# The gate products and sums of squares of one group of heads: from GpSimd to VectorE

## The chip, the cores and the metric

The kernel runs on one core of one Trainium2 chip. Times are device microseconds (us) of one execution of the whole program. The engines are TensorE (PE in the profile, its weight loads PEld), VectorE (DVE), ScalarE (ACT), GpSimd (POOL) and SyncE (SP, which here only starts transfers). Each engine runs its own list of instructions in order; semaphores make one wait for another.

## The reference, cut to what matters

A trunk of two post-norm residual layers over 16 learned tokens and 256 frames, width 2048, in float32. The first layer mixes gated linear attention and stick-breaking attention, the second is a Mamba-2 (SSD) mixer with 8 groups of 8 heads. The change lies in the second. For each group, with `y` the scan's output of 512 channels and `z` the gate path:

```python
    y = _ssd(xs, bs, cs, dt, a_log, d_skip)
    y = _rms_norm_groups(y * jax.nn.silu(z), norm_w, SSM_GROUPS)
    return jnp.einsum('bte,ed->btd', y, w_out)
...
def _rms_norm_groups(y, w, n_groups):
    yg = y.reshape(*shp[:-1], n_groups, shp[-1] // n_groups)
    yg = yg * lax.rsqrt(jnp.mean(yg * yg, -1, keepdims=True) + RMS_EPS)
    return yg.reshape(shp) * w
```

So each group needs the product of `y` with the gate, and the mean of the squares of that product over the 512 channels.

## The kernel before, in words

Everything is computed channels on partitions, tokens along the free axis. The weights are streamed from memory in units of 128 by 2048 (`load_unit`, L144, on SyncE's queue, three `raw` buffers). A unit is used as an input projection (128 output channels against 16 slices of 128 inputs) or as part of an output projection. To keep float32 accuracy on TensorE's faster path every operand is split in a high and a low part: ScalarE copies the rounded value (`whi`, L159), VectorE subtracts (`wlo`, L160; some halves on GpSimd). A unit is split in two halves into five buffers of each kind; then `in_unit` runs 16 times three matmuls (L178 to L180: high by high, low by high, high by low) into one `pj` buffer of PSUM, 48 matmuls in all. The names in the rows are `pj_9759` and so on, one number for each unit's result.

In the second layer the plan lists the units of group 0 (B, C, four x, four z), those of group 1, and then for each further group its units and the four output units of the group two before. Between the matmuls of units, work of other tasks (generators stepped by `tick`) is put in: `decay1` makes the decay matrix `M` of a group (L1125 and L1126, then an exponential, then L1153, a product with `cb`, which GpSimd's masks of L249 have made causal), `x_path` transposes x (L1193, L1197 on TensorE) and scales it to `xd` (L1206, L1212), and `mix_ssd` multiplies both (L1255, L1261 on TensorE into two `po` buffers) and makes the group's output.

In `mix_ssd`, for each of four slices of 128 channels: VectorE adds the skip term (L1265, tile `yu`), GpSimd multiplies with the gate (L1266), ScalarE makes the high part `yh` (L1268) and the square (L1271, L1274), VectorE the low part `yl` (L1269), GpSimd adds the squares up in `ysq` (L1275). TensorE then sums `ysq` over the channels (L1281, against ones, in a `po` buffer), and VectorE begins the reciprocal root with L1286. `po` has two buffers, taken in turn: two for L1255's results of a group, one for L1281, then two for L1193 of the next group, and so on.

The order of instructions on each engine is chosen when the program is built: a scheduler (the tile framework with `schedule_with_timeline_sim=True`) plays the program through with estimated times and lists instructions as they become ready; `pin` keeps some of TensorE's in program order and `high_priority` moves some ahead. So a moved instruction can move others, on all engines.

Of the kernel before, what the change touches and what calls it, by code (L numbers as in the profile page):

```python
# [9 lines left out]
ALU = mybir.AluOpType  # L10
# [72 lines left out]
def _wait(*tasks):  # L83
    for t in tasks:
        while not t.done:
            yield


class _Body:
# [1146 lines left out]
    def mix_ssd(self, g):  # L1236
        nc, lp = self.nc, self.lp
        act, vec, mm = nc.scalar.activation, nc.vector, nc.tensor.matmul
        M, xt, z = self.cur["M", g], self.cur["x", g], self.cur["z", g]
        xd = self.cur["xd", g]  # L1240
        yield from _wait(self.tasks["decay", g], *[self.tasks[a, g, j] for a in "xz" for j in (1, 3)])
        yh, yl = self.mix[g] = self.y_tiles() if g else self.y0
        sq = lp.tile([P, S], F32, tag="ysq", name=self.nm("ysq"))
        for j in range(4):
            if j == 0:
                pin = self.tc.keep_in_program_order
                for _ in range(3):
                    yield
                os = [self.po() for _ in range(2)]
                gk = dict(skip_group_check=True)  # L1250
                ov = [o.rearrange("p (j t) -> p j t", j=2) for o in os]
                for s, t0, c0, c1 in ((0, 0, 0, 256), (1, 112, 256, 400)):
                    for h in range(HPG):
                        p, jj, i = h // 4, h // 2 % 2, h % 2
                        pin(mm(  # L1255
                            ov[p][i * 64 : (i + 1) * 64, jj, t0:S], xd[:, s, h * 64 : (h + 1) * 64], M[:, h, c0:c1],
                            start=(s, jj) == (0, 0), stop=False, **gk,
                        ))
                for n in range(4):
                    p, i = n // 2, n % 2  # L1260
                    pin(mm(ov[p][i * 64 : (i + 1) * 64, :, 240:S], self.xd2[:, n, :], self.mt2[:, n], start=False, stop=True, **gk))  # L1261
                yield
            o = os[j // 2][:, (j % 2) * S : (j % 2 + 1) * S]
            u = lp.tile([P, S], F32, tag="yu", name=self.nm("yu"), bufs=2)
            vec.scalar_tensor_tensor(u, xt[:, j, NM:T], self.col(C_DS, 4 * g + j), o, op0=ALU.mult, op1=ALU.add)  # L1265
            nc.gpsimd.tensor_tensor(u, u, z[:, j, :], op=ALU.mult)  # L1266
            w = self.col(C_ON, 4 * g + j)
            act(yh[:, j, :], u, AF.Identity, scale=w)  # L1268
            vec.scalar_tensor_tensor(yl[:, j, :], u, w, yh[:, j, :].bitcast(F32), op0=ALU.mult, op1=ALU.subtract)  # L1269
            if j == 0:  # L1270
                act(sq, u, AF.Square)  # L1271
            else:
                s2 = lp.tile([P, S], F32, tag="ys2", name=self.nm("ys2"), bufs=2)
                act(s2, u, AF.Square)  # L1274
                nc.gpsimd.tensor_tensor(sq, sq, s2, op=ALU.add)  # L1275
            yield
        for _ in range(4):
            yield
        ps = self.po()
        for t in range(2):  # L1280
            mm(ps[:, 16 * t : 16 * t + 16], sq[:, t * P : (t + 1) * P], self.ones[:, :16], start=True, stop=True)  # L1281
        m = lp.tile([P, 2], F32, tag="rm", name=self.nm("rm"))
        tmp = lp.tile([P, 2], F32, tag="rt", name=self.nm("rt"))
        r = lp.tile([P, 2], F32, tag="rr", name=self.nm("rr"), bufs=3)
        self.rstd1[g] = r
        vec.tensor_scalar(m, ps[:, 0:32:16], 1.0 / 512, RMS_EPS, op0=ALU.mult, op1=ALU.add)  # L1286
        act(r, m, AF.Ln)
        act(r, r, AF.Exp, scale=-0.5)
        self.newton(r, m, tmp)
        yield  # L1290
# [188 lines left out]
```

## Time and profile before

| what | value |
|---|---|
| time, median of 3 runs (lowest, highest) | 1383.4 us (1382.73, 1383.68) |
| the profiled execution's own time | 1386.69 us |
| span of the profiled execution, first to last instruction | 1385.0 us |
| mean granted clock of TensorE | 0.998 |
| busy: TensorE, weight loads, VectorE, ScalarE, GpSimd | 99%, 96%, 74%, 55%, 19% |

The profile shows one execution. "Busy" counts instructions running; the time that an instruction spends held by another engine counts as its own. In a timeline a row can hold several like instructions (x2, x4); its duration is then from the first start to the last end. What stands in square brackets is the engine's idle time before it and what ended it. Where an engine runs back to back, the distance between two starts is the true cost of the first. Matmuls overlap: their durations are longer than the distance between their starts. [...] The second layer begins at about 680 us, group 0's output is made between about 790 and 806 us.

### The profile page before, as it was taken

How to read it: one execution, taken by the hardware profiler on the slowest of the kernel's cores; microseconds unless marked ns; L12 is line 12 of the kernel's file. 1: busy time of each engine (PE TensorE's matmuls, PEld its weight loads, DVE VectorE, ACT ScalarE, POOL GpSimd, SP SyncE). 2: the span in 40 equal slices, each digit the busy share in tenths (PEclk: the TensorE clock that was granted, in tenths of full speed). 3: DMA queues.
4: the chain of work that ended last, by engine and by line, in shares of the span. 5: the costliest groups of instructions: out<-in, count | busy, mean ns of one | idle time of the engine just before them, and what ended most of it. 6: DMA issues, size and time to landing. Idle time of an engine off the chain costs nothing.

```text
span 1385.0 us, 26232 instructions
## 1 busy us (share of the span) xinstructions
PE 1374.1 (99%) x10643; PEld 1323.9 (96%) x10643; DVE 1030.8 (74%) x1762; ACT 768.3 (55%) x1141; POOL 263.1 (19%) x253
## 2 busy tenths in 40 slices
PE   9999999999999999999999999999999999999998
PEld 8999999999999999999999999899898999989986
DVE  7858576576565674568899999787877778867687
ACT  6646455355345544556587667656565655656551
POOL 0000100100101100004401143331322323133221
PEclk9999999999999999999999999999999999999999
DMA  9656446546455545554355655465555555455561
GB/s 329 209 172 201 163 163 206 169 155 227 153 173 171 169 161 191 172 165 161 123 183 197 231 181 205 169 244 182 209 177 195 190 191 222 169 198 183 181 214 61
DMA packets 61945, 256.73 MB, mean 185 GB/s; under 512 B 26176, under 2 KB 29056, under 8 KB 33408
## 3 DMA queue, kind: packets, MB, share of 16 engines
q1 hardware_dynamic: 61104, 254.27, 53.3%
q8 instruction: 83, 1.36, 0.4%
q10 hardware_dynamic: 720, 0.79, 0.2%
q14 instruction: 38, 0.31, 0.1%
HBM read 249.29 MB, written 5.74 MB: 184 GB/s over the span
## 4 chain that ended last, share of the span: by engine, by line
PE 94%; DVE 4%; DMA 1%; issue 1%; POOL 0%; ACT 0%; SPq 0%; ACTq 0%; DVEq 0%; POOLq 0%
PE pj L179 25%; PE pj L178 25%; PE pj L180 25%; PE pj L494 4%; PE pj L496 4%; PE pj L495 4%; PE po L1255 1%; PE po L631 1%; DVE wlo L160 1%; PE po L1193 0%; DMA raw<-in_wts 0%; DVE M L1125 0%; PE z L1143 0%; DVE xt L1070 0%; DVE acc L503 0%
## 5 line engine op out<-in xcount | busy, mean ns | idle before, releaser
L178 PE MATMUL pj<-xhi,whi 128*128 128x272 f32 (+4 forms) x2560 | 732.1, 286 | 1.7 <-ACT xhi L330 0.8
L179 PE MATMUL pj<-xlo,whi 128*128 128x272 f32 (+4 forms) x2560 | 730.8, 286 | 0.0
L180 PE MATMUL pj<-xhi,wlo 128*128 128x272 f32 (+4 forms) x2560 | 730.1, 286 | 0.0
L159 ACT ACTIVATE whi<-raw 128x1024 fp32r<-128x1024 f32 (+2 forms) x434 | 449.2, 1039 | 398.3 <-PE pj L179 326.3
L160 DVE TENSOR_TENSOR wlo<-raw,whi 128x1024 fp32r<-128x1024 f32 (+2 forms) x405 | 503.4, 1247 | 209.6 <-ACT whi L159 199.6
L178 PEld LDWEIGHTS pj<-xhi,whi 128*128 128x128 f32 x2560 | 482.6, 189 | 4.3 <-ACT whi L159 1.1
L179 PEld LDWEIGHTS pj<-xlo,whi 128*128 128x128 f32 x2560 | 482.6, 189 | 1.2 <-issue 0.6
L180 PEld LDWEIGHTS pj<-xhi,wlo 128*128 128x128 f32 x2560 | 482.6, 189 | 0.8 <-issue 0.8
L178 PE MATMUL pj<-mixh,whi 128*128 128x272 f32 x384 | 111.0, 290 | 0.0
L180 PE MATMUL pj<-mixh,wlo 128*128 128x272 f32 x384 | 110.7, 289 | 0.0
L179 PE MATMUL pj<-mixl,whi 128*128 128x272 f32 x384 | 110.7, 288 | 0.0
L160 POOL TENSOR_TENSOR wlo<-raw,whi 128x1024 fp32r<-128x1024 f32 x29 | 73.1, 2520 | 193.7 <-ACT whi L159 193.7
L494 PE MATMUL pj<-whi,yh 128*128 128x512 f32 (+1 forms) x240 | 93.3, 389 | 0.0
L495 PE MATMUL pj<-wlo,yh 128*128 128x512 f32 (+1 forms) x240 | 92.6, 386 | 0.0
L496 PE MATMUL pj<-whi,yl 128*128 128x512 f32 (+1 forms) x240 | 92.2, 386 | 0.0
L261 POOL TENSOR_TENSOR gr<-gr,gsc 128x1088 f32<-128x1088 f32 x6 | 15.4, 2574 | 303.6 <-ACT gsc L260 303.6
L179 PEld LDWEIGHTS pj<-mixl,whi 128*128 128x128 f32 x384 | 72.4, 188 | 0.2
L180 PEld LDWEIGHTS pj<-mixh,wlo 128*128 128x128 f32 x384 | 72.3, 188 | 0.0
L178 PEld LDWEIGHTS pj<-mixh,whi 128*128 128x128 f32 x384 | 72.2, 188 | 0.2
L503 DVE SCALAR_TENSOR_TENSOR acc<-pj,rr,acc 128x512 f32<-128x512 f32 (+1 forms) x65 | 46.5, 733 | 13.9 <-PE pj L496 13.9
L496 PEld LDWEIGHTS pj<-whi,yl 128*128 128x128 f32 x240 | 45.1, 188 | 9.2
L494 PEld LDWEIGHTS pj<-whi,yh 128*128 128x128 f32 x240 | 45.1, 188 | 8.9
(347 smaller groups left out, 1462.4 us busy)
## 6 DMA issues: line engine op xcount, KB each, us to landing
raw<-in_wts SPq DMA_DIRECT2D x212, 1024.0 KB, 4.8
ebc<-edr SPq DMA_DIRECT2D x8, 1664.0 KB, 6.4
raw<-in_wts SPq DMA_DIRECT2D x9, 256.0 KB, 6.3
vdr<-vt SPq DMA_DIRECT2D x8, 256.0 KB, 5.2
vt<-vdr SPq DMA_DIRECT2D x32, 64.0 KB, 2.4
hacc<-in_xT SPq DMA_DIRECT2D x7, 272.0 KB, 5.3
early<-in_wts SPq DMA_DIRECT2D x2, 512.0 KB, 7.7
vdr<-vt SPq DMA_DIRECT2D x8, 128.0 KB, 3.4
```

The lines of the kernel that those rows point to most:

```text
L159: self.nc.scalar.activation(hi, src, AF.Copy)
L160: eng.tensor_tensor(lo, src, hi.bitcast(F32), op=ALU.subtract)
L178: mm(ps, whi, xhi, start=first, stop=False)
L179: mm(ps, whi, xlo, start=False, stop=False)
L180: mm(ps, wlo, xhi, start=False, stop=last)
L261: mul(c, c, e, op=ALU.mult)
L494: mm(ps, yh[:, kk, tt], hi[:, k, :], start=kk == 0, stop=False)
L495: mm(ps, yh[:, kk, tt], lo[:, k, :], start=False, stop=False)
L496: mm(ps, yl[:, kk, tt], hi[:, k, :], start=False, stop=kk == 3)
L503: self.nc.vector.scalar_tensor_tensor(a, ps, r[:, t : t + 1], a, op0=ALU.mult, op1=ALU.add)
L631: mm = lambda r, a, b, start=False, stop=False: self.nc.tensor.matmul(o[:, r], a, b, start=start, stop=stop, skip_group_check=True)
L1255: pin(mm(ov[p][i * 64 : (i + 1) * 64, jj, t0:S], xd[:, s, h * 64 : (h + 1) * 64], M[:, h, c0:c1], start=(s, jj) == (0, 0), stop=False, **gk,))
```

## The change

For group 0 of the second layer, the four gate products and the three sums of squares are issued on VectorE, with the same operands. Groups 1 to 7 keep GpSimd. The first layer is not touched: only `mix_ssd`, which belongs to the second, changes.

```diff
@@ -1263,7 +1263,8 @@
             o = os[j // 2][:, (j % 2) * S : (j % 2 + 1) * S]
             u = lp.tile([P, S], F32, tag="yu", name=self.nm("yu"), bufs=2)
             vec.scalar_tensor_tensor(u, xt[:, j, NM:T], self.col(C_DS, 4 * g + j), o, op0=ALU.mult, op1=ALU.add)
-            nc.gpsimd.tensor_tensor(u, u, z[:, j, :], op=ALU.mult)
+            side = vec if g < 1 else nc.gpsimd
+            side.tensor_tensor(u, u, z[:, j, :], op=ALU.mult)
             w = self.col(C_ON, 4 * g + j)
             act(yh[:, j, :], u, AF.Identity, scale=w)
             vec.scalar_tensor_tensor(yl[:, j, :], u, w, yh[:, j, :].bitcast(F32), op0=ALU.mult, op1=ALU.subtract)
@@ -1272,7 +1273,7 @@
             else:
                 s2 = lp.tile([P, S], F32, tag="ys2", name=self.nm("ys2"), bufs=2)
                 act(s2, u, AF.Square)
-                nc.gpsimd.tensor_tensor(sq, sq, s2, op=ALU.add)
+                side.tensor_tensor(sq, sq, s2, op=ALU.add)
             yield
```

One line is added, so line numbers behind it are one higher in the changed kernel (L1266 is L1267 there, L1281 is L1282).

The scheduler's order moves with it. On TensorE, at the place where group 0's squares are summed over the channels (`ysq_9284` into `po_9540`) and group 1's x is transposed, before the change inside the unit pj_9759 (the third z unit of group 1):

```order
 L178 MATMUL pj_9759<-xhi,whi_9726 128x256
 L179 MATMUL pj_9759<-xlo,whi_9726 128x256
-L1281 MATMUL po_9540<-ones,ysq_9284 128x16 x2
-L1193 MATMUL po_9777<-ident,xt_9353 128x128 x4
 L180 MATMUL pj_9759<-xhi,wlo_9727 128x256
```

and now inside pj_9988 (the C unit of group 2):

```order
 L178 MATMUL pj_9988<-xhi,whi_9914 128x260
 L179 MATMUL pj_9988<-xlo,whi_9914 128x260
+L1282 MATMUL po_9540<-ones,ysq_9284 128x16 x2
+L1193 MATMUL po_9777<-ident,xt_9353 128x128 x4
 L180 MATMUL pj_9988<-xhi,wlo_9915 128x260
```

The sum over the channels stands the rest of pj_9759 (7 matmuls), the 48 of pj_9853, the 48 of pj_9913 and two of pj_9988 later, and group 1's first transposes with it; the second ones and L1255 of group 1 follow some 18 matmuls behind it.

On VectorE, from the second half of pj_9759's split on (`wlo_9727`); `yu_9378`, `yu_9396`, `yu_9420` and `yu_9440` are group 0's four slices, `M_9564` is group 1's decay matrix. Before:

```order
L1070 SCALAR_TENSOR_TENSOR xt_9353<-pj_9523,cpk,xt_9353 128x271
L160 TENSOR_TENSOR wlo_9727<-raw_9612,whi_9726 128x1024
L1269 SCALAR_TENSOR_TENSOR yl_8237<-yu_9378,cpk,yh_8236 128x256
L1070 SCALAR_TENSOR_TENSOR xt_9353<-pj_9523,cpk,xt_9353 128x270
L1269 SCALAR_TENSOR_TENSOR yl_8237<-yu_9396,cpk,yh_8236 128x256
L1265 SCALAR_TENSOR_TENSOR yu_9420<-xt_8545,cpk,po_9332 128x256
L1070 SCALAR_TENSOR_TENSOR xt_9353<-pj_9523,cpk,xt_9353 128x269
L1265 SCALAR_TENSOR_TENSOR yu_9440<-xt_8545,cpk,po_9332 128x256
L1081 TENSOR_TENSOR xt_9353<-xt_9353,xcl_9471 128x544
L1077 TENSOR_SCALAR xcl_9636<-xt_9353 128x544
L160 TENSOR_TENSOR wlo_9761<-raw_9687,whi_9760 128x1024
L160 TENSOR_TENSOR wlo_9813<-raw_9687,whi_9812 128x1024
```

Now, from the sum of the first two slices' squares on:

```order
L1276 TENSOR_TENSOR ysq_9284<-ysq_9284,ys_1126_9401 128x256
L1153 TENSOR_TENSOR M_9564<-M_9564,cb_9721 128x800
L1077 TENSOR_SCALAR xcl_9636<-xt_9353 128x544
L1153 TENSOR_TENSOR M_9564<-M_9564,cb_9721 128x800 x3
L1159 TENSOR_TENSOR mt_8239<-mt,cb_9721 16x2x16
L160 TENSOR_TENSOR wlo_9813<-raw_9687,whi_9812 128x1024
L1265 SCALAR_TENSOR_TENSOR yu_9420<-xt_8545,cpk,po_9332 128x256
L1159 TENSOR_TENSOR mt_8239<-mt,cb_9721 16x2x16 x3
L1265 SCALAR_TENSOR_TENSOR yu_9440<-xt_8545,cpk,po_9332 128x256
L160 TENSOR_TENSOR wlo_9855<-raw_9757,whi_9854 128x1024
```

The product with `cb` (L1153), which stood behind both splits of the next unit, now stands ahead of the second one (`wlo_9813`) and ahead of the third and fourth slices, whose last sum of squares comes five splits L160 later still (behind `wlo_9855`, `wlo_9883`, `wlo_9915`, `wlo_9952` and `wlo_9990`). On GpSimd the seven instructions of group 0 are gone, and the three masks L249 of `cb` follow directly on the product for group 1's B and C (L1081).

## Rows read from the trace of the kernel before

**Rows 1.** The page: the busy times of part 1 (share of the span, number of instructions), and the first line of part 4, the chain that ended last by engine.

```profile
PE 1374.1 (99%) x10643; PEld 1323.9 (96%) x10643; DVE 1030.8 (74%) x1762; ACT 768.3 (55%) x1141; POOL 263.1 (19%) x253
...
PE 94%; DVE 4%; DMA 1%; issue 1%; POOL 0%; ACT 0%; SPq 0%; ACTq 0%; DVEq 0%; POOLq 0%
```

**Rows 2.** The waits of TensorE over the whole span, longest first: who waited for whom, us in total, times, longest.

```profile
PE po L1281 <- POOL ysq L1275: 2.1, 1, 2.1
PE po L1413 <- ACT diag L1348: 1.2, 1, 1.2
```

**Rows 3.** TensorE's timeline around the wait: start, duration, engine, line, operation, and the idle time before it in brackets. The first two rows are the first and last of twelve matmuls in a row, from 807.59 up to the row of 810.45 there are thirteen.

```profile
802.83 0.28 PE L180 MATMUL pj<-xhi,wlo 128*128 128x256 f32 x1
...
804.08 0.28 PE L179 MATMUL pj<-xlo,whi 128*128 128x256 f32 x1
806.41 0.62 PE L1281 MATMUL po<-ones,ysq 128*128 128x16 f32 x4 [2.06 <-POOL ysq L1275]
806.88 1.06 PE L1193 MATMUL po<-ident,xt 128*128 128x128 f32 x4
807.59 0.56 PE L180 MATMUL pj<-xhi,wlo 128*128 128x256 f32 x1
...
810.45 0.28 PE L178 MATMUL pj<-xhi,whi 128*128 128x256 f32 x1
```

**Rows 4.** Windows of 2 us: busy time and count of PE, PEld, DVE, ACT and POOL, then the granted clock of TensorE, the DMA engines' busy share and GB/s.

```profile
806.00:808.00 2.00, 1.59 (x10) 1.59 (x11) 2.00 (x2) 2.00 (x5) 0.36 (x1) 0.73 0.25 98
808.00:810.00 2.00, 2.00 (x11) 2.00 (x11) 1.95 (x8) 1.38 (x3) 0.00 (x0) 0.50 0.00 0
810.00:812.00 2.00, 2.00 (x18) 2.00 (x17) 2.00 (x5) 0.67 (x3) 0.00 (x0) 0.91 0.00 0
```

**Rows 5.** GpSimd's timeline between 740 and 806 us.

```profile
748.93 3.01 POOL L249 TENSOR_SCALAR_AFFINE_SELECT cb<-cb 128x112 f32<-128x112 f32 x3 [74.34 <-ACT cb L1146]
...
790.92 1.62 POOL L1266 TENSOR_TENSOR yu<-yu,gz 128x256 f32<-128x256 f32 x2 [20.80 <-DVE yu L1265]
794.92 1.87 POOL L1275 TENSOR_TENSOR ysq<-ysq,ys 128x256 f32<-128x256 f32 x1 [2.38 <-ACT ys L1274]
798.40 5.21 POOL L1266 TENSOR_TENSOR yu<-yu,gz 128x256 f32<-128x256 f32 x2 [1.61 <-DVE yu L1265]
803.57 0.67 POOL L249 TENSOR_SCALAR_AFFINE_SELECT cb<-cb 128x112 f32<-128x112 f32 x3
804.20 2.15 POOL L1275 TENSOR_TENSOR ysq<-ysq,ys 128x256 f32<-128x256 f32 x2
```

**Rows 6.** VectorE's timeline in the same stretch: a pair of L1153, the rows beside GpSimd's first pair of products, and the rows around the second up to the next pause.

```profile
775.42 1.87 DVE L1153 TENSOR_TENSOR M<-M,cb 128x800 f32<-128x800 f32 x2
...
791.10 0.78 DVE L1126 TENSOR_SCALAR M<-ebc,est 128x144 f32<-128x144 f32 x1
791.80 0.88 DVE L1125 TENSOR_SCALAR M<-ebc,est 128x256 f32<-128x256 f32 x1
792.61 0.28 DVE L1126 TENSOR_SCALAR M<-ebc,est 128x144 f32<-128x144 f32 x1
792.81 0.34 DVE L1125 TENSOR_SCALAR M<-ebc,est 128x256 f32<-128x256 f32 x1
...
794.55 0.48 DVE L1070 SCALAR_TENSOR_TENSOR xt<-pj,cpk,xt 128x271 f32<-128x271 f32 x1
...
798.18 0.48 DVE L1070 SCALAR_TENSOR_TENSOR xt<-pj,cpk,xt 128x269 f32<-128x269 f32 x1
798.59 0.46 DVE L1265 SCALAR_TENSOR_TENSOR yu<-xt,cpk,po 128x256 f32<-128x256 f32 x1
798.98 0.70 DVE L1081 TENSOR_TENSOR xt<-xt,xcl 128x544 f32<-128x544 f32 x1
799.62 0.42 DVE L1077 TENSOR_SCALAR xcl<-xt 128x544 f32<-128x544 f32 x1
799.97 2.34 DVE L160 TENSOR_TENSOR wlo<-raw,whi 128x1024 fp32r<-128x1024 f32 x2
804.12 4.88 DVE L1153 TENSOR_TENSOR M<-M,cb 128x800 f32<-128x800 f32 x4 [1.81 <-POOL cb L249]
```

**Rows 7.** ScalarE's timeline: the copy of `cb`, and the split of the unit after pj_9913 (the one that waited for the end of pj_9853).

```profile
797.20 0.49 ACT L1146 ACTIVATE cb<-z 128x416 f32<-128x416 f32 x1
...
815.31 1.06 ACT L159 ACTIVATE whi<-raw 128x1024 fp32r<-128x1024 f32 x1 [0.38 <-PE pj L179]
```

**Rows 8.** TensorE's timeline: the first matmul of pj_9913, transposes in its middle at full clock and the matmul behind them, and the first matmul of pj_9988.

```profile
815.23 0.29 PE L178 MATMUL pj<-xhi,whi 128*128 128x272 f32 x1
...
817.09 0.60 PE L1193 MATMUL po<-ident,xt 128*128 128x128 f32 x4
817.52 0.60 PE L1197 MATMUL z<-ident,xt 128*16 128x128 f32 x4
817.88 0.37 PE L178 MATMUL pj<-xhi,whi 128*128 128x272 f32 x1
...
822.04 0.28 PE L178 MATMUL pj<-xhi,whi 128*128 128x260 f32 x1
```

**Rows 9.** A window with another short idle time of TensorE (columns as in rows 4).

```profile
726.00:728.00 2.00, 1.54 (x13) 1.30 (x12) 2.00 (x6) 2.00 (x4) 0.00 (x0) 1.00 0.39 57
```

**Rows 10.** The page's part 6: weight loads, KB each, median us from issue to landing.

```profile
raw<-in_wts SPq DMA_DIRECT2D x212, 1024.0 KB, 4.8
```

## The prediction

> **What bounds the kernel now.** I read the page first: TensorE is busy 99% of the span and makes 94% of the chain that ended last, VectorE 4% [rows 1]. So nothing off TensorE costs time unless TensorE waits for it. Next the waits of TensorE: among all its waits the longest is one of 2.1 us, at L1281 for `ysq` from GpSimd [rows 2]. That is the sum of squares of group 0, made by exactly the instructions that the change moves. Third, TensorE's timeline there [rows 3] and the two-microsecond windows [rows 4]: the wait has a second price. TensorE stood still from about 804.3 to 806.41, and the granted clock then read 0.73, 0.50 and 0.91 in three windows before it was 1.00 again. [...]
>
> Fourth, GpSimd's timeline [rows 5] tells why `ysq` was late. A pair of gate products that took 1.62 us at 790.92 took 5.21 us at 798.40. Beside the slow pair VectorE ran a product of two SBUF tiles (L1081), L1077 and two splits (L160) with no gap [rows 6]; when VectorE stood still, from 802.3 to 804.12, the product ended, and three masks (L249) took 0.67 us together. The other direction shows too: next to the pair at 790.92 VectorE's L1126 took 0.78 us and its L1125 0.88 us, against 0.28 and 0.34 just after [rows 6]. The two engines hold each other up.
>
> **The price of the wait.** Idle: 2.06 us [rows 3]. Low clock: the thirteen matmuls from 807.59 to 810.45 took 2.86 us; at 0.114 us each, the pitch before the wait (eleven steps from 802.83 to 804.08, 1.25 us), they take 1.48, so 1.38 lost. The four transposes took 0.71 us (806.88 to 807.59) against 0.43 for four at full clock (817.09 to 817.52) [rows 3, 8]: 0.28 lost. The windows give the same: 0.27, 0.50 and 0.09 of 2 us each make 1.72 us [rows 4]. Together 2.06 + 1.7 = 3.8 us. After it TensorE waits for nothing longer than the end's 1.2 us [rows 2], so the 3.8 us would reach the end.
>
> **What the change does, step by step.** It takes seven instructions (four products, three sums, 128 by 256) off GpSimd and puts them on VectorE. On GpSimd these were 1.62 + 1.87 + 5.21 + 2.15 us [rows 5]. No row shows one on VectorE: below lies 0.30 (L1081's 0.64 us from start to start, for 544 columns, cut to 256), above 0.39 (L1265, same size, one input from PSUM) [rows 6]. I take 0.34, nearer the same operation: 2.4 us more for VectorE. Against that the 1.04 us that L1126 and L1125 lost at 791 come back.
>
> The order moves as well, as the two orders shown with the change tell. TensorE now meets L1282 not inside unit pj_9759 but after two matmuls of pj_9988. When does it get there? From 804.2: 7 matmuls left of pj_9759 and 48 of pj_9853 at 0.114 are 6.3 us; 48 of pj_9913 (272 columns) are 6.0 us (815.23 to 822.04 less 0.79 for transposes [rows 8]); two more 0.2. That is 816.7.
>
> When is the last sum of squares ready? VectorE's queue after the L1070 of 794.55 (which ends its turn at 794.96 in the profile, 793.9 with the 1.04 us back) now holds up to that sum: 7 moved at 0.34 (2.4), 8 splits L160 at 1.13 (9.0), 2 L1070 at 0.41, 2 L1081 at 0.64, 4 L1269 priced like L1265, the same kind and size (1.6), 4 L1153 at 0.93 (3.7; beside GpSimd's sums four took 4.88), 3 L1077 at 0.35 (1.1), 2 L1265 at 0.39, and six on 16 partitions, each less than L1126's 0.28 (I take 1.0), all from distances of starts and from sums in [rows 6]. The sum is 21.6 us: ready between 815.5 and 816.6, if nothing makes VectorE wait. ScalarE is not later: its split for the next unit is free when pj_9853 ends (810.5 by the count above; in the profile it waited for the same, at 815.31 [rows 7]), and after it come four copies and two short steps.
>
> So L1282 is met with 0.1 to 1.2 us to spare. It is a close thing, and the one wait in VectorE's queue decides: L1153 needs GpSimd's masks of `cb`. ScalarE hands `cb` over at 797.7 [rows 7]; VectorE arrives at L1153 at 799.4 to 800.5 by the prices above. The masks took 0.67 us beside an idle VectorE at 803.57 and 3.01 us at 748.93 [rows 5]. Hence `cb` is ready between 798.4 and 800.7, VectorE waits 0 to 1.4 us, and TensorE at L1282 0 to 1.3 us. I take 0.1, since VectorE's own standing still lets GpSimd finish, as at 803.57. A wait under 1 us need not lower the clock: 0.46 us idle in the window from 726 left it at 1.00 [rows 9].
>
> [...]
>
> The rest costs nothing that I can find. Splits: the one moved behind L1153 (wlo_9813) is done at about 805.5, while TensorE needs it 31 matmuls after 804.2, at 807.7. Group 1's operands: after L1282 TensorE has some 6 us of work (36 matmuls, two sets of transposes, half of L1255) until the second half of L1255 needs L1206's last products; VectorE has two splits, two L1206, two L1070 before them and waits for one of ScalarE's copies between, about 5 us. SyncE's weight load that waits for wlo_9813 goes out 3 us later, 5 us before use, and a load lands in 4.8 us [rows 10]: it just holds, and its split on VectorE stands behind some 8 us of other work.
>
> **Sum.** 3.8 - 0.1 = 3.7 us off. Against the profiled execution (1386.7 us, span 1385.0) that makes 1383.0; that execution lies 3.3 us above the median of the timed runs, so I put the gain on the median: 1383.4 - 3.7 = 1379.7 us.
>
> **Rivals.** (a) The wait takes a new place: GpSimd's masks are held as long as its slow product was (3.8 us beyond 797.7, so 802.2 with the masks), VectorE stands 1.7 to 2.8 us at L1153, TensorE waits about 1.5 us at L1282, with or without a short low clock. Left are 1 to 2.3 us of gain: 1381.1 to 1382.4. For it: the 5.21 us pair; against: the masks' 0.67 us once VectorE stood still.
> (b) The stall belongs to the profiled execution, which was 3.3 us longer than the median, nearly the stall's 3.8. Then nothing is there to win: 1383.4. Against: the order of instructions on each engine is fixed, and with it the neighbours that held the product.
> (c) Slower: VectorE's queue turns out over 2 us longer than my 21.6 us. Then TensorE waits at L1282 and again at L1255 of group 1, whose L1206 stands behind the same queue, each time about 2 us with its 1.7 us of low clock: 7.4 us in place of 3.8, 1387.0. It decides from 2 us on; a single such wait only breaks even. For it: VectorE was busy 1.95 to 2.00 of every 2 us here [rows 4], and was itself held by GpSimd at times [rows 6]. Against: the GpSimd products and sums that held it are gone from the stretch.
>
> **How the numbers follow.** Forecast 0.50, (a) 0.22, (b) 0.18, (c) 0.10. A measurement of this kernel tells a change from none at about 0.2%, here 2.8 us: faster means under 1380.6, slower over 1386.2. The forecast's own range is 1379.2 to 1380.6, and a little of it spills over the edge: faster 0.48; same 0.42 from (a), (b) and that spill; slower 0.10. The range from 1378.8 (no wait, and a few tenths from a freer VectorE) to 1384.0 takes in (a) and (b) and leaves (c) out.
>
> **What would show it.** Right: no wait at L1282 in TensorE's waits, the clock at 1.00 in all windows from 800 to 830, the unit after pj_9913 begun near 816.4 instead of 822.0, seven new VectorE rows near 0.4 us, and the rest of the trace shifted by 3 to 4 us. Rival (a) shows as a VectorE wait for `cb` over 2 us and a TensorE wait for `ysq` from VectorE; (b) as a trace without the wait and times unchanged; (c) as waits at L1282 and L1255 with two dips of the clock. A wait at a wlo split would show my account of VectorE's slack wrong.

## The result, and the profile after

The change made the kernel slower by 0.17%: 1384.80 us, median of 22 runs (1383.97 to 1386.59), against 1382.49 us for the kernel before, also 22 runs on the same chip (1381.61 to 1385.49). The ratio is 1.0017, with a 95% interval of 1.0011 to 1.0023, so 2.3 us more with 1.5 to 3.2 us as bounds. That is within the 0.2% that the prediction calls "same", though the interval lies wholly above 1. The profiled execution took 1384.87 us (span 1383.2 us).

The page after, as in [rows 1]: TensorE's share is what it was.

```profile
PE 1373.2 (99%) x10643; PEld 1322.9 (96%) x10643; DVE 1032.3 (75%) x1769; ACT 768.3 (56%) x1141; POOL 250.2 (18%) x246
...
PE 94%; DVE 3%; DMA 1%; ACT 1%; issue 1%; POOL 0%; SPq 0%; ACTq 0%; POOLq 0%; DVEq 0%
```

GpSimd has seven instructions less and VectorE seven more, as the diff says. TensorE's waits, as in [rows 2] (who waited for whom, us, times, longest):

```profile
PE pj L178 <- ACT gz L1222: 1.3, 1, 1.3
PE po L1414 <- ACT diag L1349: 1.2, 1, 1.2
...
PE po L1282 <- POOL ysq L1276: 0.6, 1, 0.6
```

The wait of 2.06 us that the change was to remove is gone. In its place stand two that the trace of before did not have: 1.3 us at the first matmul of pj_9913, for ScalarE's copy of z from PSUM to the tile `gz` (L1222), and 0.6 us at L1282, which is group 1's and not group 0's. TensorE's timeline, to be held against [rows 3] and [rows 8] (this trace runs about 1 us earlier there than that of before; each trace has its own start):

```profile
809.35 0.28 PE L180 MATMUL pj<-xhi,wlo 128*128 128x256 f32 x1
810.93 0.39 PE L178 MATMUL pj<-xhi,whi 128*128 128x272 f32 x1 [1.30 <-ACT gz L1222]
...
817.55 0.52 PE L1282 MATMUL po<-ones,ysq 128*128 128x16 f32 x4
817.92 0.63 PE L1193 MATMUL po<-ident,xt 128*128 128x128 f32 x4
...
844.87 0.62 PE L1282 MATMUL po<-ones,ysq 128*128 128x16 f32 x4 [0.61 <-POOL ysq L1276]
```

Group 0's sum over the channels (817.55) starts without a wait. The windows around the new wait, as in [rows 4] and [rows 9], show that it does not lower the clock: TensorE is idle for 0.38 us of the first window and 0.93 of the second, and the granted clock (a share of full speed) reads 1.00 in both.

```profile
808.00:810.00 2.00, 1.62 (x15) 1.42 (x13) 2.00 (x5) 1.27 (x3) 0.00 (x0) 1.00 0.70 176
810.00:812.00 2.00, 1.07 (x8) 1.08 (x9) 2.00 (x5) 2.00 (x7) 0.00 (x0) 1.00 0.85 356
```

VectorE's timeline, as in [rows 6]: the first row is a pair of moved products, then the sum of squares ahead of L1153 and L1153 itself, the last two products, and the last sum.

```profile
792.93 0.74 DVE L1267 TENSOR_TENSOR yu<-yu,gz 128x256 f32<-128x256 f32 x2
793.60 1.21 DVE L160 TENSOR_TENSOR wlo<-raw,whi 128x1024 fp32r<-128x1024 f32 x1
...
798.11 0.41 DVE L1276 TENSOR_TENSOR ysq<-ysq,ys 128x256 f32<-128x256 f32 x1
798.71 0.99 DVE L1153 TENSOR_TENSOR M<-M,cb 128x800 f32<-128x800 f32 x1 [0.19 <-POOL cb L249]
...
808.11 0.42 DVE L1267 TENSOR_TENSOR yu<-yu,gz 128x256 f32<-128x256 f32 x1
...
809.78 0.41 DVE L1267 TENSOR_TENSOR yu<-yu,gz 128x256 f32<-128x256 f32 x1
...
814.32 0.40 DVE L1276 TENSOR_TENSOR ysq<-ysq,ys 128x256 f32<-128x256 f32 x1
```

A moved product costs 0.33 us (0.67 us from the pair's start to the next row). The last product of group 0 now ends at 810.19. ScalarE's timeline, as in [rows 7], says who waits for it:

```profile
809.54 1.06 ACT L159 ACTIVATE whi<-raw 128x1024 fp32r<-128x1024 f32 x1 [0.17 <-PE pj L179]
810.51 1.19 ACT L1222 ACTIVATE gz<-pj 128x256 f32<-128x256 f32 x4
```

All four copies of group 1's z run together at 810.51. The tile `gz` has one buffer, and group 0's last product reads it until 810.19; so no copy of group 1's z may write it before. As long as no copy has run, four results of z units lie in the four `pj` buffers of PSUM, and the next unit (pj_9913) has nowhere to write. On ScalarE the split whi_9989 (809.54) now stands ahead of all four copies, so TensorE waits for the split and the copy; in the kernel before three copies stood ahead of that split. (The scheduler may have put it there because by its estimates the product comes late; no run shows its reason.) GpSimd's timeline explains the other wait, as in [rows 5] (there the stretch ends at 806):

```profile
796.85 1.96 POOL L249 TENSOR_SCALAR_AFFINE_SELECT cb<-cb 128x112 f32<-128x112 f32 x3 [27.70 <-ACT cb L1146]
...
834.50 2.77 POOL L160 TENSOR_TENSOR wlo<-raw,whi 128x1024 fp32r<-128x1024 f32 x1 [1.53 <-ACT whi L159]
838.48 1.71 POOL L1267 TENSOR_TENSOR yu<-yu,gz 128x256 f32<-128x256 f32 x2 [1.21 <-DVE yu L1265]
842.70 2.12 POOL L1276 TENSOR_TENSOR ysq<-ysq,ys 128x256 f32<-128x256 f32 x2 [2.51 <-ACT ys L1275]
```

The scheduler now lists a split (wlo_10216) ahead of group 1's last two products; before it stood behind them. The two waits, 1.30 and 0.61 us, are 1.9 of the 2.3 us, within the bounds of 1.5 to 3.2.

### The profile page after: what moved, and what is told of

Its sections match the earlier page's. It is cut to its first block, busy times and chain, and to the rows that moved or that the text cites. A ratio compares the mean times of both kernels' runs of the same rounds, so it can differ in the third digit from the quotient of the medians.

```text
span 1383.2 us, 26230 instructions
## 1 busy us (share of the span) xinstructions
PE 1373.2 (99%) x10643; PEld 1322.9 (96%) x10643; DVE 1032.3 (75%) x1769; ACT 768.3 (56%) x1141; POOL 250.2 (18%) x246
## 4 chain that ended last, share of the span: by engine, by line
PE 94%; DVE 3%; DMA 1%; ACT 1%; issue 1%; POOL 0%; SPq 0%; ACTq 0%; POOLq 0%; DVEq 0%
PE pj L179 25%; PE pj L178 25%; PE pj L180 25%; PE pj L494 4%; PE pj L496 4%; PE pj L495 4%; PE po L1255 2%; PE po L631 1%; DMA raw<-in_wts 1%; PE po L1193 1%; DVE M L1125 0%; PE z L1143 0%; DVE M L1126 0%; DVE acc L503 0%; DVE wlo L160 0%
## 5 line engine op out<-in xcount | busy, mean ns | idle before, releaser
L160 DVE TENSOR_TENSOR wlo<-raw,whi 128x1024 fp32r<-128x1024 f32 (+2 forms) x405 | 503.9, 1248 | 204.6 <-ACT whi L159 199.2
L160 POOL TENSOR_TENSOR wlo<-raw,whi 128x1024 fp32r<-128x1024 f32 x29 | 73.4, 2529 | 194.2 <-ACT whi L159 194.2
L494 PE MATMUL pj<-whi,yh 128*128 128x512 f32 (+1 forms) x240 | 93.3, 389 | 0.0
L496 PE MATMUL pj<-whi,yl 128*128 128x512 f32 (+1 forms) x240 | 92.4, 387 | 0.0
L496 PEld LDWEIGHTS pj<-whi,yl 128*128 128x128 f32 x240 | 45.1, 188 | 9.1
L494 PEld LDWEIGHTS pj<-whi,yh 128*128 128x128 f32 x240 | 45.1, 188 | 8.9
```

Source lines behind the costliest of these rows:

```text
L160: eng.tensor_tensor(lo, src, hi.bitcast(F32), op=ALU.subtract)
L494: mm(ps, yh[:, kk, tt], hi[:, k, :], start=kk == 0, stop=False)
L496: mm(ps, yl[:, kk, tt], hi[:, k, :], start=False, stop=kk == 3)
```

## The experiments

Theory A: the late place of group 0's last product costs the 1.3 us, through the one z buffer, ScalarE's copies and the PSUM buffers. Its rival, theory B: the seven instructions load a VectorE that had no time left. A second question stands beside them: where are the 3.8 us that were to be won? All kernels here compute the whole reference. An edge (`add_manual_dep` in the diffs) tells the scheduler to list one instruction behind another on the same engine; it adds no semaphore. The diffs are cut, with `...` where lines are left out; `gate0`, `gate1`, `copy0` and `copies` keep the instructions that an edge names. Added lines shift line numbers by up to 8: the copy of z is then L1225 or L1226, the product L1270 to L1274. The first four kernels ran together on one chip with 33 runs of the kernel before (median 1382.69 us); the next three and "The other wait mended" with 32 (1382.56); "Three copies late", "A second z tile" and the changed kernel once more with 27 (1382.66). Each had 11 runs, one had 10. "Above before" is the distance of these medians; the ratio's interval, in brackets, is about 1.2 us to either side.

**The kernel before, once more.** No edit.

> The kernel before, unchanged, for a second trace of it. Theory A (the long wait at L1281 with its low clock is the exception, since most timed runs of before lie near 1382 us and two near 1385.4): no window with a granted clock under 1.00 near 806 us, the wait at L1281 under 1.5 us, span near 1381. Theory B (the wait and the low clock are in every run): again about 2 us of wait, a window at 0.5, span near 1385. Timed: ratio 1.000 by both.

Measured: 1382.19 us, ratio 0.9999 (0.999 to 1.0007). The profile of this execution (span 1380.0 us) shows the same place on TensorE so:

```profile
803.17 0.62 PE L1281 MATMUL po<-ones,ysq 128*128 128x16 f32 x4 [0.21 <-POOL ysq L1275]
```

and on GpSimd so:

```profile
789.51 4.94 POOL L1266 TENSOR_TENSOR yu<-yu,gz 128x256 f32<-128x256 f32 x2 [20.79 <-DVE yu L1265]
795.38 0.76 POOL L1275 TENSOR_TENSOR ysq<-ysq,ys 128x256 f32<-128x256 f32 x1 [0.93 <-ACT ys L1274]
796.09 0.75 POOL L1266 TENSOR_TENSOR yu<-yu,gz 128x256 f32<-128x256 f32 x1
797.16 1.01 POOL L1266 TENSOR_TENSOR yu<-yu,gz 128x256 f32<-128x256 f32 x1 [0.32 <-POOL yu L1266]
```

The same program, but here the first pair of products is the slow one (4.94 us, 1.62 in [rows 5]) and the second is not (0.75 and 1.01 us, 5.21 for both there). The first has slack, the second has none: TensorE waits 0.21 us in place of 2.06, and the clock stays at 1.00. So the stall is not in every execution. Of 114 timed runs of the kernel before in the four comparisons 7 took over 1385 us and none the 1386.69 us of the profiled one; of the 92 whose clock is on record 3 had its mean granted clock of 0.998.

**Each half of the change alone.** The sums on VectorE, the products left on GpSimd:

```diff
+            side = vec if g < 1 else nc.gpsimd
...
-                nc.gpsimd.tensor_tensor(sq, sq, s2, op=ALU.add)
+                side.tensor_tensor(sq, sq, s2, op=ALU.add)
```

> Only the three sums of squares of group 0 on VectorE, the products on GpSimd. Theory A (the change loses because group 0's last product, late in VectorE's queue, holds the only buffer of z; group 1's copies out of PSUM, L1222, then come behind a split on ScalarE, and pj_9913 waits for its PSUM buffer): the copies of pj_9614 and pj_9689 stand ahead of whi_9882 here, so no wait at L178 for gz, and the time is that of before or less, 1381 to 1383 us. Theory B (VectorE's added work as such): about three sevenths of the loss, 1383.5 us.

Measured: 1382.35 us, ratio 1.000 (0.999 to 1.0009), and no wait for `ysq` or `gz`. The products alone:

```diff
-            nc.gpsimd.tensor_tensor(u, u, z[:, j, :], op=ALU.mult)
+            side = vec if g < 1 else nc.gpsimd
+            side.tensor_tensor(u, u, z[:, j, :], op=ALU.mult)
```

> Only the four gate products of group 0 on VectorE, the sums on GpSimd. Theory A (z's buffer and the copies behind the split): the copy of pj_9614 stands behind whi_9989 as in the changed kernel, so again about 1.3 us of wait at L178 for gz and 1384 to 1385 us. Theory B (VectorE's added work): four sevenths of the loss, 1383.8 us, with no particular wait at L178.

Measured: 1383.86 us, ratio 1.0009 (1.0 to 1.0017), 1.2 us above before. TensorE's timeline has the wait of the changed kernel to the hundredth:

```profile
810.56 0.39 PE L178 MATMUL pj<-xhi,whi 128*128 128x272 f32 x1 [1.30 <-ACT gz L1222]
```

The one at group 1's sum is not there. The products carry the 1.3 us; the sums by themselves cost nothing that can be measured.

**The products early.** The whole change, with the split wlo_9855 on VectorE listed behind group 0's last product:

```diff
+            if (g, j) == (0, 3):
+                self.gate0 = self.traced()[-1]
...
+            if (n, h) == (20, 0):
...
+                self.tc.add_manual_dep(self.traced()[-1], self.gate0.name, free, reason="gate_first")
```

> The changed kernel, with one order edge: VectorE's split wlo_9855 comes behind group 0's last product, which brings the products 3 splits forward and the copies of pj_9614, pj_9689 and pj_9759 ahead of whi_9989 on ScalarE. Same work on every engine. Theory A: no wait at L178 for gz, 1.3 us less than the changed kernel, 1383.0 to 1383.8 us. Theory B (VectorE's added work): same time as the changed kernel, 1384.8.

Measured: 1382.86 us, ratio 1.0003 (0.9994 to 1.0012). VectorE has the same seven instructions to do, the last product at 806.67:

```profile
806.67 0.41 DVE L1270 TENSOR_TENSOR yu<-yu,gz 128x256 f32<-128x256 f32 x1
```

Three of the four copies run ahead of the split whi_9989 again:

```profile
808.79 0.91 ACT L1225 ACTIVATE gz<-pj 128x256 f32<-128x256 f32 x3
...
810.29 1.06 ACT L159 ACTIVATE whi<-raw 128x1024 fp32r<-128x1024 f32 x1
```

Both new waits are gone, and the loss with them. (One other wait of TensorE is new, 0.45 us at 869.96 for group 2's x; the time does not show it.) Theory B wanted the time of the changed kernel, 2.3 us above before. The load of VectorE costs nothing that can be measured; theory B falls.

**The copies ahead of the split.** The next four take the chain apart. First, in the changed kernel, the split on ScalarE behind the copies, VectorE left alone:

```diff
+        if (g, j) == (1, 0):
+            self.copy0 = self.traced()[-1]
...
+            if (n, h) == (22, 0):
...
+                self.tc.add_manual_dep(self.traced()[-2], self.copy0.name, free, reason="copy_first")
```

> The changed kernel with one edge: on ScalarE the split whi_9989 stands behind group 1's first z copy (L1222 from pj_9614), so the four copies run as soon as group 0's last product on VectorE is done. Theory A (the z tile's single buffer ties TensorE to that product): in the changed kernel the product ends at about 810.2, the end of pj_9853 is at 809.63, the split holds the copy until 810.51. With the edge the copy starts at 810.2 and takes 0.3: TensorE's wait for pj_9614 shrinks from 1.3 to about 0.9 us, not to zero; the time falls by about 0.4 us against the changed kernel, to some 1.5 to 1.9 us above before. Rival (the wait is all the split's): it goes to 0.3 us or less. Rival B (VectorE's greater load costs the time): the wait may go, the time stays 2.3 us above before.

Measured: 1384.08 us, ratio 1.001 (1.0001 to 1.0018), 1.5 us above before. TensorE waits 1.05 us, and ScalarE's row names the product as what it waited for:

```profile
811.87 1.21 ACT L1225 ACTIVATE gz<-pj 128x256 f32<-128x256 f32 x4 [0.84 <-DVE yu L1272]
```

The split made up only 0.25 us of the wait. Without it the product is still late. (The wait at group 1's sum is not in this profile, nor in the next: the edges moved that order too.)

**The product later still.** The changed kernel, with group 0's last product one split (wlo_9952) further down VectorE's list:

```diff
+            if (n, h) == (21, 1):
...
+                self.tc.add_manual_dep(self.gate0, self.traced()[-1].name, free, reason="gate_late")
...
```

> The changed kernel with one edge: group 0's last product on VectorE stands behind one split more (wlo_9952, 1.13 us). Theory A: the product ends at 811.3 instead of 810.2, the copy follows at once (the split of ScalarE ends at 810.6, no longer the last thing), so TensorE's wait for pj_9614 grows from 1.3 to about 2.1 us, and the time by 0.8 us, to about 3.1 us above before; if a wait of this length also lowers the clock, by up to 1.7 us more. Rival (the split on ScalarE alone sets the wait): 1.3 us, as in the changed kernel, and no change of time.

Measured: 1386.17 us (10 runs), ratio 1.0021 (1.0011 to 1.003), 3.6 us above before. The wait grew to 2.17 us:

```profile
812.85 0.39 PE L181 MATMUL pj<-xhi,whi 128*128 128x272 f32 x1 [2.17 <-ACT gz L1225]
```

and, the windows behind it show, the clock fell:

```profile
812.00:814.00 2.00, 1.15 (x7) 1.15 (x8) 2.00 (x6) 1.59 (x6) 0.00 (x0) 0.84 0.84 238
814.00:816.00 2.00, 2.00 (x11) 2.00 (x11) 1.78 (x5) 1.73 (x6) 0.00 (x0) 0.50 0.94 393
816.00:818.00 2.00, 2.00 (x15) 2.00 (x15) 0.00 (x0) 0.96 (x2) 0.00 (x0) 0.80 0.10 41
```

One split of 1.13 us moved the wait by 0.87 us, as theory A said. The three windows lost 0.32, 1.00 and 0.40 us to the lower clock, 1.7 in all, by the way of counting that the prediction used on [rows 4]. Seven of the ten runs, between 1385.8 and 1387.2 us, had a mean clock of 0.998, as the profiled execution of before had; the other three, between 1384.3 and 1385.5 us, had 0.999 or more.

**One copy late, without the change.** The kernel before, with the copy from pj_9614 alone behind the split whi_9989:

```diff
+            if (n, h) == (22, 0):
...
+                self.tc.add_manual_dep(self.copy0, self.traced()[-2].name, free, reason="copy_late")
...
```

> The kernel before, nothing on VectorE, with one edge: the z copy of group 1 from pj_9614 stands behind the split whi_9989 on ScalarE, as in the changed kernel. Theory A: TensorE waits at the first matmul of pj_9913 for 1.0 us of split and 0.3 us of copy, 1.3 us in all, and the time rises by 1.3 us above before (1.0 to 1.6). Rival B (the products' load or the moved order on VectorE costs the time): no change, 0.3 us at most.

Measured: 1382.71 us, ratio 1.0003 (0.9994 to 1.0012). The expectation missed: the copy is as late as it was to be, but TensorE does not wait. ScalarE's timeline:

```profile
802.34 0.35 ACT L1225 ACTIVATE gz<-pj 128x256 f32<-128x256 f32 x1
...
806.63 0.36 ACT L1225 ACTIVATE gz<-pj 128x256 f32<-128x256 f32 x1
...
811.32 1.06 ACT L159 ACTIVATE whi<-raw 128x1024 fp32r<-128x1024 f32 x1 [0.91 <-PE pj L182]
812.29 0.64 ACT L1225 ACTIVATE gz<-pj 128x256 f32<-128x256 f32 x2
```

TensorE's:

```profile
811.12 0.28 PE L183 MATMUL pj<-xhi,wlo 128*128 128x256 f32 x1
811.24 0.29 PE L181 MATMUL pj<-xhi,whi 128*128 128x272 f32 x1
```

The copies of the second and third z unit ran at 802.34 and 806.63, and pj_9913 begins at 811.24, a microsecond before the copy from pj_9614. So a unit does not take the buffers in turn; one that is free is enough. The changed kernel waits because none of the four copies may run.

**Three copies late, without the change.** As the last, with the edge on the copies from pj_9614, pj_9689 and pj_9759:

```diff
+            if (n, h) == (22, 0):
...
+                for late in self.copies:
+                    self.tc.add_manual_dep(late, self.traced()[-2].name, free, reason="copy_late")
...
```

> The kernel before with edges that put three of group 1's z copies (from pj_9614, pj_9689 and pj_9759) behind the split whi_9989 on ScalarE; the fourth stands there anyway. Nothing is on VectorE. If the first matmul of pj_9913 takes whichever pj buffer is free first (as the run with one late copy suggests), TensorE now waits there 1.0 us for the split and 0.3 us for a copy, 1.3 us, and the time is 1.0 to 1.6 us above before. If the moved products' load or place on VectorE is what costs, no change.

Measured: 1383.43 us, ratio 1.0004 (0.9995 to 1.0013), 0.8 us above before, less than expected. TensorE's timeline shows why:

```profile
815.48 0.60 PE L1197 MATMUL po<-ident,xt 128*128 128x128 f32 x4
815.92 0.60 PE L1201 MATMUL z<-ident,xt 128*16 128x128 f32 x4
816.95 0.40 PE L182 MATMUL pj<-xhi,whi 128*128 128x272 f32 x1 [0.43 <-ACT gz L1226]
```

The edge also moved group 1's second transposes in between pj_9853 and pj_9913; they fill 0.9 us, and 0.43 of the 1.3 remain as a wait for `gz`. That confirms the way from the copies to TensorE without the change, at a size that the comparison alone can't tell from nothing. (This profile happened on the long stall again: 2.28 us at group 0's sum, with the second pair of products at 5.21 us.)

**The other wait mended.** The change, with GpSimd's split wlo_10216 behind group 1's last product:

```diff
+            if (g, j) == (1, 3):
+                self.gate1 = self.traced()[-1]
...
+            if (n, h) == (24, 1):
...
+                self.tc.add_manual_dep(self.traced()[-1], self.gate1.name, free, reason="split_late")
```

> The changed kernel with one edge: GpSimd's split wlo_10216 stands behind group 1's last product, as in the kernel before. Theory A: the wait of 0.6 us at group 1's L1282 for GpSimd's sums is gone, the one of 1.3 us for the z copy stays; the time falls by about 0.6 us against the changed kernel, to about 1.7 us above before. Rival: the 0.6 us is covered or comes back elsewhere, and the time stays 2.3 us above before.

Measured: 1384.11 us, ratio 1.0011 (1.0003 to 1.002), 1.55 us above before. The wait at group 1's sum is gone, the one of 1.30 us stays, and the time is 0.7 to 0.8 us nearer to before than that of the changed kernel. So the two waits add, as far as medians tell: the intervals overlap.

**A second z tile.** The change, with group 1's z in one of the two `yl` tiles, which is not yet in use then:

```diff
+            if g == 1:
+                self.cur["z", g] = self.lp.tile([P, 4, S], F32R, tag="yl", name=self.nm("gz"), bufs=2).bitcast(F32)
```

> The changed kernel with a z tile of its own for group 1 (it takes one of the two yl tiles, which nobody uses yet at that time), so that group 1's z copies (L1222, here L1225) no longer wait for group 0's last product. Theory A: although that product is as late on VectorE as in the changed kernel, TensorE's wait for a gz copy at the first matmul of pj_9913 goes from 1.3 us to 0.2 us or less, and the time falls by 1.0 to 1.9 us against the changed kernel (the freed copies move other instructions too, the wait of 0.6 us at group 1's sum among them), to 0.4 to 1.3 us above before. Rival: the wait stays, since it is ScalarE's order and not the tile that ties the copy.

Measured: 1382.61 us, ratio 1.0 (0.9991 to 1.0008). On VectorE the last product is no earlier than in the changed kernel:

```profile
810.38 0.41 DVE L1270 TENSOR_TENSOR yu<-yu,gz 128x256 f32<-128x256 f32 x1
```

ScalarE has by then copied three of group 1's four z results, the first 12.5 us earlier:

```profile
797.85 0.35 ACT L1225 ACTIVATE gz<-pj 128x256 f32<-128x256 f32 x1
...
799.89 0.36 ACT L1225 ACTIVATE gz<-pj 128x256 f32<-128x256 f32 x1
...
805.33 0.36 ACT L1225 ACTIVATE gz<-pj 128x256 f32<-128x256 f32 x1
```

and TensorE starts pj_9913 without a wait:

```profile
809.72 0.29 PE L178 MATMUL pj<-xhi,whi 128*128 128x272 f32 x1
```

The z buffer is what tied TensorE to the late product. The order of instructions moved as well (group 1's sum stands later on TensorE), and the wait of 0.6 us went with it, so all 2.3 us came back, more than the 1.0 to 1.9 expected.

**The changed kernel, once more.** No edit, beside the last two.

> The changed kernel once more, beside the two others on the same chip: the waits of 1.3 us for the z copy and of 0.6 us at group 1's L1282 stand in the profile again, since both follow from the order of instructions, and the time is 2.3 us above before (1.7 to 2.7).

Measured: 1384.93 us, ratio 1.0015 (1.0006 to 1.0024), 2.27 us above before, with both waits at 1.3 and 0.6 us. So both stand in both profiles of the changed kernel, and all of its 33 timed runs lie above 1383.8 us: the waits go with the order of the instructions, unlike the stall of before.

No version here beats the kernel before by more than can be measured: with the early products or the second tile the time is the same.

## Why the prediction was wrong

It said 1379.7 us, and 1378.8 to 1384.0 as range; measured were 1384.80. Two steps failed.

**The price of the wait**, 2.06 us idle and 1.7 us of low clock. Both numbers were read rightly from the profile, but the sum took 3.8 us off the median of timed runs, and few of those can hold the stall: 7 of 114 took over 1385 us. Rival (b) had said so and been given 0.18, against the argument that "the order of instructions on each engine is fixed, and with it the neighbours that held the product". The order is fixed; which pair is slow within it is not, as the second profile of the same program shows (0.75 and 1.01 us where the first had 5.21). The evidence stood in the prediction itself: the profiled execution was 3.3 us above the median, nearly the whole stall. In the second profile there was 0.2 us to win, too little to be measured; the median of the timed runs (1382.5 us, that profile's own time 1381.7) suggests that most executions are like it.

**"The rest costs nothing that I can find."** That step asked for the splits, group 1's operands and a weight load, but not for the tile that the moved product reads. The order had put the product behind two further splits; after it the prediction priced only what follows in its own chain, `yh`, the square and the sum. It even counted "four copies and two short steps" on ScalarE behind pj_9853's end, as a delay for `ysq`, without asking why four copies should stand there together and what waits for them. They free PSUM. Measured: 1.3 us. The same step missed GpSimd's list for group 1, where a split went ahead of two products: 0.6 us.

The other steps held. VectorE's queue from the turn's end of L1070 (792.93 in this trace) to the end of the last sum (814.72) is 21.8 us, predicted 21.6; the moved instructions cost 0.33 us each, predicted 0.34; L1153 waits 0.19 us for `cb`, predicted 0 to 1.4, which refutes rival (a); TensorE reaches L1282 2.8 us after the sum is ready, 1.3 of that owed to the new wait, so 1.5 without it, a little over the 0.1 to 1.2 predicted; no window there has a lower clock. Rival (c) had the right sign by another mechanism: VectorE's queue was not too long.

GpSimd's masks of `cb`, on which rival (a) rested, were slow as well, at no cost to TensorE. In the changed kernel the three took 1.96 us, 1.3 more than beside an idle VectorE [rows 5], and one of them alone 1.59 us, from 797.09 to 798.68, where all three took 0.67 there. Beside it VectorE ran no split but L1070, two of L1270 and L1276, each under 0.5 us, up to 798.52; L1153 waited only 0.19 us for `cb`. The slow products of before ran beside several VectorE instructions too: of the pair of 5.21 us the first ran from 798.40 to 802.92, beside all five that [rows 6] shows from 798.59 on, and the second took 0.74 us. They differ by 3.8 us, the price that rival (a) took.

## What to carry to other kernels

When an instruction moves later, ask not only who reads its result but who wants to overwrite what it reads: with one buffer, the next writer, everything that the writer empties (here PSUM) and the engine that fills it all move with it. Before a stall is priced, see whether the profiled execution is longer than the timed ones by as much; then it may be that execution's own, and a second profile of the same program tells. And where a scheduler orders the instructions, read the moved order for every engine, in the next stage too: of the 1.9 us found here, 0.6 lay 27 us behind the place of the change.

A gap on TensorE that came only once, of 1.3 us, meant one buffer too few here, as the second z tile shows.

## What the runs showed of the hardware

One and the same pair of GpSimd products took 5.21 us in one execution of a program and 1.76 us (0.75 and 1.01) in another, and the pair before it 1.62 and 4.94 us; VectorE ran the same list beside them both times, and one of the two pairs was slow in each. GpSimd's product L1081, 1.29 us in the changed kernel, took 7.14 us with the second z tile, where it ran 8 us earlier beside a VectorE that was busy without a gap until 816.1, three splits among its work; nobody waited for it:

```profile
810.17 7.14 POOL L1081 TENSOR_TENSOR gz<-gz,xcl 128x512 f32<-128x512 f32 x1 [11.09 <-ACT xcl L1080]
```

How the two patterns of the kernel before come about from one execution to the next was not tried.

On TensorE's granted clock: waits of 1.30 and 0.61 us in the changed kernel, and of 1.30 us where the products alone were moved, left it at 1.00 in the windows around them; waits of 2.06, 2.17 and 2.28 us (before, the product later still, three copies late) were each followed by a window at 0.50 in the profiled execution. Between 4 and 1378 us no window of 2 us in the trace of before, other than the three of [rows 4], and none in that of the changed kernel shows less than 1.00. By the windows the lower clock cost 1.7 us after each of the first two and 3.4 us after the third (0.56, 1.00, 1.00 and 0.86 of 2 us each), of which these are the first two and the last:

```profile
804.00:806.00 2.00, 1.14 (x6) 1.14 (x7) 2.00 (x3) 2.00 (x4) 0.81 (x1) 0.72 0.46 184
806.00:808.00 2.00, 2.00 (x11) 2.00 (x10) 2.00 (x5) 0.55 (x2) 0.00 (x0) 0.50 0.00 0
...
810.00:812.00 2.00, 2.00 (x13) 2.00 (x12) 2.00 (x5) 0.00 (x0) 0.00 (x0) 0.57 0.00 0
```

They are from the kernel before with three copies late, whose profiled execution took 1387.8 us, 4.4 above the median of its runs. So a wait's cost can jump: between the change with GpSimd's list mended (1.30 us at pj_9913 and no other new wait) and the change with the product later still (2.17 us there, and no wait at group 1's sum either) lie 0.87 us of wait and 2.1 us of time (1384.11 and 1386.17).

What the split of the operands is for shows in the trace of before, at a clock of 1.00: an unsplit float32 product of 256 columns (L1405, two records) took 0.43 us, from its start to the next one's (1374.77 to 1375.20), and each of the split products of 256 columns just ahead of it (L494 to L496) 0.12 us.
